# Condition tiles loaded a step ahead from GpSimd's queue, and gate one-hots built for eight tokens per instruction, in a three-layer transformer kernel

## The chip, the core and the metric

The kernel runs on one core of a Trainium2 chip. The core has a matrix engine (TensorE, PE in the rows), a vector engine (VectorE, DVE), an engine for activation functions (ScalarE, ACT), GpSimd (POOL), and SyncE (SP), which here issues most of the transfers. Each engine runs its own instructions in the order in which they stand. They wait for each other through semaphores. The metric is the device time of one execution in microseconds (us), and the median of several executions is the kernel's time.

## What is computed

Three layers run over 256 tokens of width 1024. The first two take a gain, a shift and a gate from a condition vector `c`, and the third ends in a product-key expert layer. Cut to what matters:

```python
cond = jax.nn.silu(c)
for i in range(2):
    mod = (cond @ ada_w[i] + ada_b[i]).reshape(B, 6, D)      # 6144 numbers per layer
    h = rms_norm(x, norm_mix[i]) * (1 + scale1) + shift1
    x = x + gate1 * (mla_mixer(h) if i == 0 else dilated_mixer(h))
    h = rms_norm(x, norm_mlp[i]) * (1 + scale2) + shift2
    x = x + gate2 * (jnp.square(jax.nn.relu(h @ mlp_w1[i])) @ mlp_w2[i])
# third layer: recurrence and chunk attention, cross attention, then the experts:
#   8 heads pick 16 of 16384 experts each, number = 128 * i1 + i2, gate = softmax of the scores
act = gelu(einsum('td,tkd->tk', x, expert_u[idx]))
x = x + einsum('tk,tkd->td', gate * act, expert_v[idx])
```

## The kernel before

Weights come from memory as slabs of 128 x 1024 float32 (`slab`, line 264): SP loads a slab into `raw` (4 buffers), ScalarE rounds it to `wH` (line 268), VectorE takes the rest `wL = raw - wH` (line 270), and TensorE multiplies with three matmuls per 128 x 128 block (`mm3`, lines 275 to 277). A linear step of 1024 inputs and 128 outputs is one slab and 24 matmuls. An engine can be at most four slabs ahead, since `raw`, `wH` and `wL` have four buffers each.

**Condition tiles.** `cond @ ada_w` is not done on TensorE. The transposed weights lie as 48 tiles of 128 x 1024 per layer (512 KB each). One tile gives 128 of the 6144 numbers: `ada_tile` (line 458) loads the tile into `araw`, multiplies it with `cond` (the same in every row) and sums along the row. That is one instruction on VectorE (line 465), or, for tiles marked `pool_too`, a multiply on GpSimd (line 462) and a summing copy on ScalarE (line 463). There are 96 tiles. The first 16 are worked off in the start, with 8 buffers of their own. The other 80 share two `araw` buffers and are handed out as "aside" steps: 24 in the latent attention (`mla`, half of them through GpSimd), 24 in the first MLP (all but one on VectorE), 24 in the dilated attention (`dil`, half through GpSimd) and 8 in the second MLP (half). Their loads go through `late` (line 259), which puts a load on SP's queue and tells the scheduler to keep it behind the slab that was asked for last. Load and sum of a tile are written in one step.

Beside these tiles the first MLP also hides the bias tables of `dil` (`t5`, line 788): 20 transfers `br` issued by GpSimd bring bucket numbers in, VectorE compares them (`oh`, line 853), TensorE looks the bias up (lines 861, 862), and ScalarE's queue stores it.

**Experts.** All 128 x 128 expert columns are computed densely. `up(n2)` is one slab of `expert_u`: 24 matmuls and a gelu. The gates are spread out to a 128 x 128 table per token by a matmul of two one-hot matrices: for each token t and each of the 128 selections, `A` marks the first key number and `B` holds the gate at the second key number, in two float16 parts. This *build* goes over 4 quarters of 64 tokens and in each over 8 chunks of 8 tokens (`TC = 8`): 24 small VectorE instructions per chunk (lines 1532 and 1534), 16 matmuls (line 1539), two evictions into `G` (line 1540). A finished quarter is stored to memory in 8 pieces from ScalarE's queue (line 1547). `fill(us)` places `up` steps into the build: one per 1.5 of the sum of its arguments. Then follows the *value stage*: gate pieces `GG` are loaded back (line 1565), and `gw`, `gaH`, `gaL` (lines 1575 to 1580) are multiplied with slabs of `expert_v` into `v`. Its first matmul needs the stored gates of all four quarters.

**Order.** The program is written as nested loops, but a scheduler that keeps a model of the timing picks the order of the instructions on each engine, within the bounds of dependences, buffers and such hints as `late`. Once built, the order is fixed: an instruction that waits holds up everything behind it on its engine.

Of the kernel before, what the change touches and what calls it, by code (L numbers as in the profile page):

```python
# [11 lines left out]
F32 = mybir.dt.float32  # L12
F32R = mybir.dt.float32r
BF = mybir.dt.bfloat16
F16 = mybir.dt.float16
# [6 lines left out]
T = 256  # L22
# [197 lines left out]
def program(ctx: ExitStack, tc, I, out, co):  # L220
# [234 lines left out]
                nc.tensor.matmul(p[:, k], sel[:, 512 * n + 128 * k:512 * n + 128 * k + 128], e, start=True, stop=True)  # L455
            evict(cond[:, 512 * n:512 * n + 512], p.rearrange("p a b -> p (a b)"))

    def ada_tile(l, j, pool_too=False, tp=None, bufs=2, behind=False):
        raw = (tp or ada_pool).tile([128, 1024], F32, name="araw", bufs=bufs)
        (late if behind else dma)(raw, I["adaT"][l, j])  # L460
        if pool_too:
            nc.gpsimd.tensor_tensor(raw, raw, cond, op=OP.mult)  # L462
            nc.scalar.activation(raw, raw, AF.Copy, accum_out=MOD[l][:, j:j + 1])
            return
        nc.vector.tensor_tensor_reduce(raw, raw, cond, scale=1.0, scalar=0.0, op0=OP.mult, op1=OP.add,  # L465
                                       accum_out=MOD[l][:, j:j + 1])

    def ada_end(l, part):
        s = slice(8 * part, 8 * part + 8)
        nc.vector.tensor_add(MOD[l][:, s], MOD[l][:, s], cc(f"ada_b{l}", 8 * part, 8))  # L470
        if part % 3 == 1:
            n = ("norm_mix", "norm_mlp")[part // 3]
            o = slice(8 * (part // 3), 8 * (part // 3) + 8)
            nc.vector.scalar_tensor_tensor(GA[l][:, o], MOD[l][:, s], 1.0, cc(f"{n}{l}", 0, 8),
                                           op0=OP.add, op1=OP.mult)

    def ada_steps(l, parts, pool_of=2):
        for part in parts:
            for j in range(8 * part, 8 * part + 8):
                ada_tile(l, j, j % pool_of == 0, behind=True)  # L480
                if j % 8 == 7:
                    ada_end(l, part)
                yield

    def mod_normed(l, half):
        with pool("psn", space=PS) as pn:
# [134 lines left out]
    def mla(sin, cos, X, r):  # L621
        with pool("mla") as mp:
# [3 lines left out]
            with pool("mlap") as lp, pool("psacc", 5, space=PS) as pa, pool("psss", space=PS) as ps:  # L626
# [8 lines left out]
                kr = lp.tile([128, T], F32, name="kr")  # L635
                XQ = [lp.tile([128, 3, T], F32R, name="xq" + s) for s in "HL"]
                XK = [lp.tile([128, 2, T], F32R, name="xk" + s) for s in "HL"]
                tiles = iter(range(16, 40))

                def aside(n):  # L640
                    for _ in range(n):
                        j = next(tiles, None)
                        if j is None:
                            return
                        ada_tile(0, j, j % 2 == 0, behind=True)
                        if j % 8 == 7:
                            ada_end(0, j // 8)

                w = I["w_mla_in"]
                for m in (3, 4, 0, 1, 2):  # L650
# [714 lines left out]
    def peer(Xq, done):  # L1365
# [11 lines left out]
        X = normed(xt, 8, r, lambda k: cc("norm_ffn", k), pair())  # L1377
        pre.close()
        with pool("peer") as mp, pool("psp", 2, space=PS) as ps:
            iT = [mp.tile([128, T], F32, name=f"iT{j}") for j in range(3)]  # L1380
            g16 = mp.tile([128, T], F16, name="g16")
            gp = [mp.tile([128, T], F32, name=f"gp{j}") for j in range(2)]
            iota = mp.tile([128, 128], F16, name="iota")
            io = mp.tile([128, 128], F32, name="io")
            dma(io, I["iota"])
# [31 lines left out]
            with pool("route") as rp, pool("psr", space=PS) as pr:  # L1417
# [51 lines left out]
                def gates(t):  # L1469

                    e = got[t][2].rearrange("p (a b) -> p a b", a=8)
                    nc.vector.tensor_sub(e, tops[t], tops[t][:, :, 0:1].to_broadcast([128, 8, 16]))
                    nc.scalar.activation(e, e, AF.Exp)
                    su = rp.tile([128, 8], F32, name="su", bufs=2)
                    nc.vector.reduce_sum(su, e, axis=AX.X)
                    nc.vector.reciprocal(su, su)
                    nc.vector.tensor_mul(e, e, su[:, :, None].to_broadcast([128, 8, 16]))
                    s = slice(128 * t, 128 * t + 128)
                    for j in range(3):
                        p = pr.tile([128, 128], F32, name="tr", bufs=1)  # L1480
                        nc.tensor.transpose(p, got[t][j], ident)
                        nc.scalar.activation(iT[j][:, s], p, AF.Copy, scale=(1.0, 1.0, 2.0 ** 15)[j])

                    nc.vector.tensor_copy(g16[:, s], iT[2][:, s])
                    nc.vector.tensor_copy(gp[0][:, s], g16[:, s])
                    nc.vector.tensor_sub(gp[1][:, s], iT[2][:, s], gp[0][:, s])
                    fill(1.5)

# [34 lines left out]
            with pool("build") as bt, pool("psb", space=PS) as pb:  # L1523
                for q in range(NQ):
                    G = bt.tile([128, 128, TQ], F32, name="G", bufs=2)
                    for c in range(TQ // TC):
                        A = bt.tile([128, TC, 128], F16, name="A", bufs=2)
                        B = bt.tile([128, TC, 2, 128], F16, name="Bg", bufs=2)
                        for j in range(TC):
                            t = TQ * q + TC * c + j  # L1530
                            col = lambda v: v[:, t:t + 1]
                            nc.vector.tensor_scalar(A[:, j], iota, col(iT[0]), None, op0=OP.is_equal)
                            for i in range(2):
                                nc.vector.tensor_scalar(B[:, j, i], iota, col(iT[1]), col(gp[i]), op0=OP.is_equal, op1=OP.mult)  # L1534
                        for j in range(0, TC, TP):
                            p = pb.tile([128, TP, 128], F32, name="gb", bufs=4)
                            for k in range(TP):
                                for i in range(2):
                                    nc.tensor.matmul(p[:, k], A[:, j + k], B[:, j + k, i], start=i == 0, stop=i == 1)
                            nc.scalar.activation(G[:, :, TC * c + j:TC * c + j + TP], p.rearrange("p t n -> p n t"), AF.Copy,  # L1540
                                                 scale=2.0 ** -15)
                        if stores:
                            stores.pop(0)()
                        fill(3.7)

                    def store(q, G, n):
                        return lambda: nc.scalar.dma_start(gd[q, :, n:n + SN], G[:, n:n + SN])  # L1547

                    stores += [store(q, G, n) for n in range(0, 128, SN)]
                for n2 in todo:  # L1550
                    up(n2)
                    if stores:
                        stores.pop(0)()
                while stores:
                    stores.pop(0)()
# [90 lines left out]
    with pool("start") as start:  # L1646
# [3 lines left out]
        def between():  # L1650
            k = next(n)
            for j in (k, 8 + k):
                ada_tile(0, j, j < 8, start, 8)
                nc.vector.tensor_add(MOD[0][:, j:j + 1], MOD[0][:, j:j + 1], cc("ada_b0", j))
            nc.vector.scalar_tensor_tensor(GA[0][:, k:k + 1], MOD[0][:, 8 + k:9 + k], 1.0, cc("norm_mix0", k),
                                           op0=OP.add, op1=OP.mult)
# [47 lines left out]
```

## Time and profile before

| | us |
|---|---|
| median of 3 executions | 2071.1 (2070.01 to 2071.22) |
| the profiled execution | 2070.24 |
| its span, from the first instruction to the last | 2068.5 |
| TensorE busy in the span | 1945.3 (94%) |
| VectorE busy | 1582.8 (77%) |
| ScalarE busy | 1195.7 (58%) |
| GpSimd busy | 194.5 (9%) |

Busy shares are averages over stages of different kinds. Matmuls overlap, so a busy TensorE need not run at its peak. A stage is judged by what TensorE waits for in it, and by the engine that is behind that wait. Windows below are in us from the start of the span. The latent attention and its output end at about 222, the first MLP runs to about 457, `dil` to about 830, the second MLP begins there, the build runs from 1410 to 1663, and the value stage from about 1697 to the end.

### The profile page before, as it was taken

How to read it: one execution, taken by the hardware profiler on the slowest of the kernel's cores; microseconds unless marked ns; L12 is line 12 of the kernel's file. 1: busy time of each engine (PE TensorE's matmuls, PEld its weight loads, DVE VectorE, ACT ScalarE, POOL GpSimd, SP SyncE). 2: the span in 40 equal slices, each digit the busy share in tenths (PEclk: the TensorE clock that was granted, in tenths of full speed). 3: DMA queues.
4: the chain of work that ended last, by engine and by line, in shares of the span. 5: the costliest groups of instructions: out<-in, count | busy, mean ns of one | idle time of the engine just before them, and what ended most of it. 6: DMA issues, size and time to landing. Idle time of an engine off the chain costs nothing.

```text
span 2068.5 us, 36918 instructions
## 1 busy us (share of the span) xinstructions
PE 1945.3 (94%) x13516; PEld 1755.7 (85%) x13516; DVE 1582.8 (77%) x3606; ACT 1195.7 (58%) x2270; POOL 194.5 (9%) x156
## 2 busy tenths in 40 slices
PE   6988998888999999999999999999999979999998
PEld 5765998887878787999987999998899968888886
DVE  8877885547776876875588679999999947777676
ACT  4855676335775675695466565554455535555554
POOL 4112111111221210300100110000000000000000
PEclk8998999999999999999999999999999989999999
DMA  8663588777645643665554545554677788888674
GB/s 322 224 224 112 205 252 242 252 249 238 227 163 166 204 133 102 233 198 190 190 198 134 204 144 174 179 173 155 246 242 246 275 284 283 293 292 287 226 243 143
DMA packets 170247, 441.91 MB, mean 214 GB/s; under 512 B 20705, under 2 KB 74745, under 8 KB 169425
## 3 DMA queue, kind: packets, MB, share of 16 engines
q1 hardware_dynamic: 158064, 409.99, 59.8%
q10 hardware_dynamic: 6480, 24.12, 3.0%
q0 software_dynamic: 5520, 5.44, 1.1%
q8 instruction: 106, 1.74, 0.3%
q14 instruction: 77, 0.62, 0.1%
HBM read 398.40 MB, written 37.91 MB: 211 GB/s over the span
## 4 chain that ended last, share of the span: by engine, by line
PE 71%; DMA 9%; DVE 9%; ACT 4%; issue 3%; ACTq 1%; SPq 0%; POOL 0%; DVEq 0%; POOLq 0%
PE acc L275 16%; PE acc L277 15%; PE acc L276 15%; DMA araw<-in_adaT 6%; PE v L275 6%; PE v L276 6%; PE v L277 6%; DVE wL L270 3%; ACT wH L268 1%; ACTq L1547 1%; DVE Bg L1534 1%; DVE araw L465 1%; PE S L938 1%; PE acc L921 1%; PE acc L590 1%
## 5 line engine op out<-in xcount | busy, mean ns | idle before, releaser
L268 ACT ACTIVATE wH<-raw 128x1024 fp32r<-128x1024 f32 x565 | 595.8, 1058 | 443.9 <-PE acc L276 285.6
L270 DVE TENSOR_TENSOR wL<-raw,wH 128x1024 fp32r<-128x1024 f32 x565 | 700.7, 1245 | 176.8 <-ACT wH L268 157.1
L275 PE MATMUL acc<-hH,wH 128*128 128x256 f32 (+1 forms) x2168 | 628.6, 290 | 15.4 <-ACT gs L1401 7.8
L276 PE MATMUL acc<-hL,wH 128*128 128x256 f32 (+1 forms) x2168 | 619.6, 286 | 5.9 <-DVE hL L394 5.3
L277 PE MATMUL acc<-hH,wL 128*128 128x256 f32 (+1 forms) x2168 | 616.6, 285 | 1.8 <-DVE wL L270 1.8
L275 PEld LDWEIGHTS acc<-hH,wH 128*128 128x128 f32 x2168 | 413.9, 191 | 24.8 <-ACT gs L1401 9.5
L276 PEld LDWEIGHTS acc<-hL,wH 128*128 128x128 f32 x2168 | 413.1, 191 | 9.1 <-DVE hL L394 6.1
L277 PEld LDWEIGHTS acc<-hH,wL 128*128 128x128 f32 x2168 | 412.7, 191 | 3.9 <-DVE wL L270 2.5
L275 PE MATMUL v<-wH,gaH 128*128 128x512 f32 x512 | 200.4, 391 | 13.3 <-ACT gaH L1579 13.3
L276 PE MATMUL v<-wL,gaH 128*128 128x512 f32 x512 | 200.2, 391 | 0.0
L277 PE MATMUL acc<-hidH,wL 128*128 128x256 f32 x512 | 146.4, 286 | 11.0 <-DVE wL L270 11.0
L465 DVE CUSTOM_DVE_ANT_0 araw<-araw,cond 128x1024 f32<-128x1024 f32 x59 | 83.5, 1416 | 95.2 <-DMA araw<-in_adaT 95.2
L275 PE MATMUL acc<-hidH,wH 128*128 128x256 f32 x512 | 145.6, 284 | 1.0 <-ACT wH L268 1.0
L276 PE MATMUL acc<-hidL,wH 128*128 128x256 f32 x512 | 145.6, 284 | 0.0
L277 PE MATMUL v<-wH,gaL 128*128 128x512 f32 x512 | 140.7, 390 | 0.0
L1534 DVE TENSOR_SCALAR Bg<-iota,iT,gp 128x128 f16<-128x128 f16 x512 | 138.5, 309 | 0.0
L462 POOL TENSOR_TENSOR araw<-araw,cond 128x1024 f32<-128x1024 f32 x37 | 92.7, 2506 | 350.7 <-DMA araw<-in_adaT 301.4
L275 PEld LDWEIGHTS v<-wH,gaH 128*128 128x128 f32 x512 | 96.7, 189 | 33.4 <-ACT gaH L1579 13.5
L1579 ACT ACTIVATE gaH<-gw 128x256 fp32r<-128x256 f32 x128 | 53.4, 418 | 115.7 <-PE v L276 97.4
L277 PEld LDWEIGHTS v<-wH,gaL 128*128 128x128 f32 x512 | 96.6, 189 | 20.3
L276 PEld LDWEIGHTS v<-wL,gaH 128*128 128x128 f32 x512 | 96.7, 189 | 19.9
L277 PEld LDWEIGHTS acc<-hidH,wL 128*128 128x128 f32 x512 | 98.8, 193 | 12.4 <-DVE wL L270 12.2
(447 smaller groups left out, 3385.5 us busy)
## 6 DMA issues: line engine op xcount, KB each, us to landing
raw<-in_w SPq DMA_DIRECT2D x128, 512.0 KB
raw<-in_uT SPq DMA_DIRECT2D x128, 512.0 KB
raw<-in_v SPq DMA_DIRECT2D x128, 512.0 KB
araw<-in_adaT SPq DMA_DIRECT2D x96, 512.0 KB
gd<-G ACTq DMA_DIRECT2D x32, 512.0 KB
GG<-gd SPq DMA_DIRECT2D x32, 512.0 KB
raw<-in_w_dv SPq DMA_DIRECT2D x24, 512.0 KB
raw<-in_w_dq SPq DMA_DIRECT2D x24, 512.0 KB
```

The lines of the kernel that those rows point to most:

```text
L268: nc.scalar.activation(H, raw, AF.Copy)
L270: (lo or nc.vector).tensor_sub(L, raw, H)
L275: kept(nc.tensor.matmul(p, aH, bH, start=start, stop=False))
L276: kept(nc.tensor.matmul(p, aH, bL, start=False, stop=False))
L277: kept(nc.tensor.matmul(p, aL, bH, start=False, stop=stop))
L462: nc.gpsimd.tensor_tensor(raw, raw, cond, op=OP.mult)
L465: nc.vector.tensor_tensor_reduce(raw, raw, cond, scale=1.0, scalar=0.0, op0=OP.mult, op1=OP.add, accum_out=MOD[l][:, j:j + 1])
L590: nc.tensor.matmul(p, KB[:v[i].shape[0], 128 * j:128 * j + 128], v[i], start=i == 0, stop=i == 1)
L921: nc.tensor.matmul(p[:, 1], k2("b64"), square(p[:, 0]), start=True, stop=True)
L938: nc.tensor.matmul(Ss[i][:, t], pm(q[rows], t), kt, start=True, stop=True)
L1534: nc.vector.tensor_scalar(B[:, j, i], iota, col(iT[1]), col(gp[i]), op0=OP.is_equal, op1=OP.mult)
L1579: nc.scalar.activation(aH, w, AF.Copy)
```

## The change

The load of a tile and its sum become two functions. `ada_steps` asks for the load of the next tile before it sums the present one, and issues it from GpSimd's queue, no longer through `late`. The handing out in `mla` now goes through `ada_steps` too. The 16 tiles of the start stay on SP's queue.

In the build the 24 instructions of a chunk become four over all eight tokens (8 x 128 elements): two comparisons and two products. In each, one operand is a token's number or gate, repeated along the innermost dimension. The tiles `iT` and `gp` become float16 where they were float32, and a helper tile is dropped. `fill` is given 2.8 per chunk in place of 3.7.

```diff
-    def ada_tile(l, j, pool_too=False, tp=None, bufs=2, behind=False):
+    def ada_load(l, j, tp=None, bufs=2, q=None):
         raw = (tp or ada_pool).tile([128, 1024], F32, name="araw", bufs=bufs)
-        (late if behind else dma)(raw, I["adaT"][l, j])
+        (q or dma)(raw, I["adaT"][l, j])
+        return raw
+
+    def ada_sum(l, j, raw, pool_too=False):
         if pool_too:
             nc.gpsimd.tensor_tensor(raw, raw, cond, op=OP.mult)
             nc.scalar.activation(raw, raw, AF.Copy, accum_out=MOD[l][:, j:j + 1])
...
     def ada_steps(l, parts, pool_of=2):
-        for part in parts:
-            for j in range(8 * part, 8 * part + 8):
-                ada_tile(l, j, j % pool_of == 0, behind=True)
-                if j % 8 == 7:
-                    ada_end(l, part)
-                yield
+
+        js = [j for part in parts for j in range(8 * part, 8 * part + 8)]
+        raw = {}
+        for n, j in enumerate(js):
+            for k in js[n:n + 2]:
+                if k not in raw:
+                    raw[k] = ada_load(l, k, q=nc.gpsimd.dma_start)
+            ada_sum(l, j, raw[j], j % pool_of == 0)
+            if j % 8 == 7:
+                ada_end(l, j // 8)
+            yield
...
-                tiles = iter(range(16, 40))
+                tiles = ada_steps(0, (2, 3, 4))
...
-            iT = [mp.tile([128, T], F32, name=f"iT{j}") for j in range(3)]
-            g16 = mp.tile([128, T], F16, name="g16")
-            gp = [mp.tile([128, T], F32, name=f"gp{j}") for j in range(2)]
+            iT = [mp.tile([128, T], F16 if j < 2 else F32, name=f"iT{j}") for j in range(3)]
+            gp = [mp.tile([128, T], F16, name=f"gp{j}") for j in range(2)]
...
-                        for j in range(TC):
-                            t = TQ * q + TC * c + j
-                            col = lambda v: v[:, t:t + 1]
-                            nc.vector.tensor_scalar(A[:, j], iota, col(iT[0]), None, op0=OP.is_equal)
-                            for i in range(2):
-                                nc.vector.tensor_scalar(B[:, j, i], iota, col(iT[1]), col(gp[i]), op0=OP.is_equal, op1=OP.mult)
+                        s = slice(TQ * q + TC * c, TQ * q + TC * c + TC)
+                        inner = lambda v: v[:, s, None].to_broadcast([128, TC, 128])
+                        numbers = iota[:, None, :].to_broadcast([128, TC, 128])
+                        eq = bt.tile([128, TC, 128], F16, name="eqb", bufs=1)
+                        nc.vector.tensor_tensor(A, numbers, inner(iT[0]), op=OP.is_equal)
+                        nc.vector.tensor_tensor(eq, numbers, inner(iT[1]), op=OP.is_equal)
+                        for i in range(2):
+                            nc.vector.tensor_tensor(B[:, :, i], eq, inner(gp[i]), op=OP.mult)
...
-                        fill(3.7)
+                        fill(2.8)
```

The built order moves with it, since loads are no longer held behind slabs. In the first MLP GpSimd's queue before held the bucket transfers in a row (`br`), after one condition sum:

```order
L462 TENSOR_TENSOR araw<-araw,cond 128x1024
L832 DMA buck_d_2417<-bb 128x384
L833 DMA buck_d_2418<-bb 128x256
L849 DMA br<-buck_d_2417 128x1x1024 x12
L849 DMA br<-buck_d_2418 128x1x1024 x5
L386 TENSOR_TENSOR ssq<-ssq,sq 128x256
```

The same place now (`L460` is a tile's load, `L465` a tile's multiply on GpSimd):

```order
L835 DMA buck_d_2419<-bb 128x384
L836 DMA buck_d_2420<-bb 128x256
L460 DMA araw<-in_adaT 128x1024
L465 TENSOR_TENSOR araw<-araw,cond 128x1024
L852 DMA br<-buck_d_2419 128x1x1024 x3
L460 DMA araw<-in_adaT 128x1024 x2
L852 DMA br<-buck_d_2419 128x1x1024 x2
L465 TENSOR_TENSOR araw<-araw,cond 128x1024
L852 DMA br<-buck_d_2419 128x1x1024
L460 DMA araw<-in_adaT 128x1024 x2
```

Loads and multiplies of tiles now stand among the bucket transfers. The tiles that `dil` and the second MLP handed out have moved into the first MLP, and no tile is left behind its 55th slab or so. On VectorE in the latent attention there was one condition sum (`L465`) in every two or three heads, among the softmax steps (`mx`, `ng`, `sums`, `P`):

```order
L565 TENSOR_REDUCE mx<-acc 128x2
L567 TENSOR_SCALAR ng<-mx 128x2
L574 RECIPROCAL sums<-sums 128x2
L465 ISA araw,mod_92<-araw,cond 128x1024
L465 ISA mod_92 128x1
L576 TENSOR_SCALAR P<-P,sums 128x256 x2
L565 TENSOR_REDUCE mx<-acc 128x2
L574 RECIPROCAL sums<-sums 128x2
L363 TENSOR_TENSOR xqL<-o,xqH 128x256
```

There now (`L468` is the sum):

```order
L468 ISA araw,mod_92<-araw,cond 128x1024
L468 ISA mod_92 128x1
L573 TENSOR_REDUCE mx<-acc 128x2
L468 ISA araw,mod_92<-araw,cond 128x1024
L468 ISA mod_92 128x1
L575 TENSOR_SCALAR ng<-mx 128x2
L573 TENSOR_REDUCE mx<-acc 128x2
L582 RECIPROCAL sums<-sums 128x2
L575 TENSOR_SCALAR ng<-mx 128x2
L584 TENSOR_SCALAR P<-P,sums 128x256 x2
L573 TENSOR_REDUCE mx<-acc 128x2
L468 ISA araw,mod_92<-araw,cond 128x1024
```

From the first `mx` to the first row of the output projection there were 6 sums, and now there are 20: those of the first MLP have moved here. On VectorE in the build the row was of small instructions with a `wL` among them:

```order
L270 TENSOR_TENSOR wL<-raw,wH 128x1024
L1532 TENSOR_SCALAR A<-iota,iT_14121 128x128
L1534 TENSOR_SCALAR Bg<-iota,iT_14122,gp_14125 128x128
L1534 TENSOR_SCALAR Bg<-iota,iT_14122,gp_14126 128x128
L1532 TENSOR_SCALAR A<-iota,iT_14121 128x128
```

and is now

```order
L1534 TENSOR_TENSOR A<-iota,iT_14121 128x1024
L1537 TENSOR_TENSOR Bg<-eqb,gp_14124 128x8x128
L1537 TENSOR_TENSOR Bg<-eqb,gp_14125 128x8x128
L270 TENSOR_TENSOR wL<-raw,wH 128x1024
L1535 TENSOR_TENSOR eqb<-iota,iT_14122 128x1024
L270 TENSOR_TENSOR wL<-raw,wH 128x1024
```

Two `wL` stand in most chunks, where before it was two or three.

## Rows read from the trace of the kernel before

**Rows 1.** The page, its first part: busy time, share of span, instructions.

```profile
PE 1945.3 (94%) x13516; PEld 1755.7 (85%) x13516; DVE 1582.8 (77%) x3606; ACT 1195.7 (58%) x2270; POOL 194.5 (9%) x156
```

**Rows 2.** Windows by stage: length; PE, PEld, DVE, ACT, POOL busy; clock; DMA; GB/s.

```profile
0.00:57.00 57.00, 36.83 (x202) 32.91 (x202) 50.32 (x87) 30.90 (x57) 21.29 (x16) 0.85 0.82 311
...
222.00:457.00 235.00, 212.98 (x1606) 204.55 (x1605) 158.70 (x244) 130.35 (x248) 27.61 (x31) 0.95 0.78 248
...
475.00:830.00 355.00, 345.37 (x2248) 289.43 (x2249) 261.30 (x646) 238.13 (x565) 66.93 (x51) 0.97 0.52 171
...
1410.00:1663.00 253.00, 242.38 (x2188) 234.66 (x2187) 238.50 (x842) 124.33 (x203) 0.00 (x0) 0.99 0.68 233
1663.00:1701.00 38.00, 24.72 (x193) 23.58 (x192) 11.77 (x15) 12.35 (x22) 0.00 (x0) 0.83 0.90 324
```

**Rows 3.** VectorE's waits in the whole span: total, times, longest.

```profile
DVE araw L465 <- DMA araw<-in_adaT: 95.2, 30, 8.6
```

**Rows 4.** VectorE's waits in the first MLP, 222 to 457.

```profile
DVE araw L465 <- DMA araw<-in_adaT: 67.7, 15, 8.6
```

**Rows 5.** Timeline of SP and of VectorE, 355 to 400: start, duration, what.

```profile
357.02 0.42 SPq L262 DMA_DIRECT2D araw<-in_adaT  x1
...
368.16 1.23 DVE L465 CUSTOM_DVE_ANT_0 araw<-araw,cond 128x1024 f32<-128x1024 f32 x1 [8.62 <-DMA araw<-in_adaT]
```

**Rows 6.** The chain that ended last: start, duration, what. Loads in it.

```profile
167.23 5.84 DMA araw<-in_adaT
...
440.88 9.01 DMA araw<-in_adaT
...
466.81 5.97 DMA araw<-in_adaT
...
839.59 5.99 DMA araw<-in_adaT
```

**Rows 7.** Groups of instructions by line (busy us, mean ns | idle before, releaser).

```profile
L462 POOL TENSOR_TENSOR araw<-araw,cond 128x1024 f32<-128x1024 f32 x37 | 92.7, 2506 | 350.7 <-DMA araw<-in_adaT 301.4 <-ACT P L571 17.8 <-ACT mnH L1262 9.3
L463 ACT ACTIVATE araw<-araw 128x1024 f32<-128x1024 f32 x37 | 39.0, 1054 | 31.0 <-POOL araw L462 31.0
L849 POOL DMA_DIRECT2D br<-buck_d x20 | 13.6, 683 | 95.9 <-DVE oh L853 84.9 <-DMA br<-buck_d 7.6 <-issue 3.3
```

**Rows 8.** DMA issues: queue, count, size, median us from issue to landing.

```profile
br<-buck_d POOLq DMA_DIRECT2D x20, 256.0 KB, 11.9
```

**Rows 9.** One tile, `araw`: duration ns min/median/max, first and last start.

```profile
L465 DVE CUSTOM_DVE_ANT_0 araw<-araw,cond x59: 1208/1226/3405, 14.7 to 862.2; 128x1024 f32<-128x1024 f32 x59
```

**Rows 10.** Shorter windows, columns as in rows 2: start, attention and after it.

```profile
30.00:40.00 10.00, 3.33 (x24) 2.93 (x24) 9.86 (x20) 4.72 (x6) 5.35 (x3) 0.81 1.03 408
...
140.00:200.00 60.00, 46.48 (x197) 29.48 (x198) 48.25 (x114) 35.19 (x105) 14.08 (x6) 0.83 0.50 163
200.00:210.00 10.00, 10.00 (x65) 8.07 (x62) 1.18 (x4) 1.53 (x5) 0.00 (x0) 0.83 0.01 2
```

**Rows 11.** Timeline of VectorE inside the build.

```profile
1505.95 1.22 DVE L270 TENSOR_TENSOR wL<-raw,wH 128x1024 fp32r<-128x1024 f32 x1
1507.09 0.25 DVE L1532 TENSOR_SCALAR A<-iota,iT 128x128 f16<-128x128 f16 x1
1507.25 0.53 DVE L1534 TENSOR_SCALAR Bg<-iota,iT,gp 128x128 f16<-128x128 f16 x2
1507.70 0.24 DVE L1532 TENSOR_SCALAR A<-iota,iT 128x128 f16<-128x128 f16 x1
```

**Rows 12.** Two other VectorE lines: of 1024 elements each.

```profile
L1462 DVE TENSOR_TENSOR eq<-ra,const x4: 1218/1219/1223, 1287.2 to 1384.9; 128x1024 f32<-128x1024 f32 x4
...
L853 DVE TENSOR_SCALAR oh<-br,const 128x1024 fp32r<-128x1024 bf16 x20 | 15.4, 772 | 3.1 <-DMA br<-buck_d 3.0
```

**Rows 13.** A window of `up` steps alone on TensorE, columns as in rows 2.

```profile
1250.00:1300.00 50.00, 50.00 (x421) 50.00 (x420) 48.88 (x236) 24.70 (x42) 0.00 (x0) 1.00 0.56 180
```

**Rows 14.** TensorE's waits, 1663 to 1705: total, times, longest.

```profile
PE v L275 <- ACT gaH L1579: 13.3, 1, 13.3
```

More of the change, by code (lines that the diff above doesn't have):

```diff
@@ L637, in mla @@
                 XK = [lp.tile([128, 2, T], F32R, name="xk" + s) for s in "HL"]
-                tiles = iter(range(16, 40))
+                tiles = ada_steps(0, (2, 3, 4))
                 def aside(n):
                     for _ in range(n):
[L642 to L647, printed above, removed]
+                        next(tiles, None)
                 w = I["w_mla_in"]
@@ L1482, in gates @@
                         nc.scalar.activation(iT[j][:, s], p, AF.Copy, scale=(1.0, 1.0, 2.0 ** 15)[j])
-                    nc.vector.tensor_copy(g16[:, s], iT[2][:, s])
-                    nc.vector.tensor_copy(gp[0][:, s], g16[:, s])
+                    nc.vector.tensor_copy(gp[0][:, s], iT[2][:, s])
                     nc.vector.tensor_sub(gp[1][:, s], iT[2][:, s], gp[0][:, s])
@@ L1652, in between @@
             for j in (k, 8 + k):
-                ada_tile(0, j, j < 8, start, 8)
+                ada_sum(0, j, ada_load(0, j, start, 8), j < 8)
                 nc.vector.tensor_add(MOD[0][:, j:j + 1], MOD[0][:, j:j + 1], cc("ada_b0", j))
```

## The prediction

> **What bounds the kernel now.** I read the page's busy times first, then the windows by stage, then the waits in each stage, then the chain that ended last, and single rows last. TensorE is busy 94% of the span [rows 1], so a change gains only where TensorE idles, where its clock is low, or where it works slower than it could behind another engine. In the first MLP it is busy 213.0 of 235 us at clock 0.95; in `dil` 345.4 of 355; in the build 242.4 of 253; between build and value stage 24.7 of 38 [rows 2]. VectorE waits for condition tiles 95.2 us in 30 waits [rows 3], 67.7 of them in 15 waits in the first MLP [rows 4]. One such wait in full: SP issues the load at 357.02, and VectorE stands 8.62 us in front of the sum until 368.16 [rows 5]. Every `wL` behind that sum is late by as much. That the waits reach TensorE shows in the chain: four loads of tiles lie on it, one in the attention (5.84), one late in the first MLP (9.01), one at the start of `dil` (5.97) and one at the start of the second MLP (5.99) [rows 6]. In the build VectorE is busy 238.5 of 253 us [rows 2], almost as full as TensorE.
>
> The sum is made against the profiled execution (2070.24, of which the span is 2068.5); the median of the runs, 2071.1, lies 0.9 above it.
>
> **Start: +7 (0 to +13).** The built order draws some six loads of tiles, two or three sums on VectorE and three multiplies on GpSimd into the start. Where the start is full the transfers run at 1.03 of their share and 408 GB/s, and VectorE is busy 9.86 of 10 us [rows 10]. Six loads of 524 KB at 408 GB/s are 6 x 1.28 = 7.7 us; I take 7. Over all 57 us the share is 0.82 [rows 2], so they may fit in at nothing; three sums beside GpSimd, at somewhere between the median 1.23 and the longest 3.41 [rows 9], could add some 5 more.
>
> **Latent attention: +6 (-4 to +20).** It gets 14 sums more on VectorE (20 for 6), 14 x 1.23 = 17 us [rows 9]. VectorE idles 11.7 of 60 us in the attention and 8.8 of 10 behind it [rows 10]. With 20 as the upper end (17 and 3 of delay between them), I let a third show, since VectorE there works between short waits of the softmax; without its load on the chain (5.84 [rows 6]) it could gain 4.
>
> **First MLP: -7 (-33 to +47).** It loses 23 sums on VectorE with their waits, and gets the 32 tiles of `dil` and the second MLP, as 16 pairs, 15 of them between its 35th and 87th slab counted from the kernel's first; the bucket transfers `br` stand among 9 of these. A pair is one tile for VectorE and one for GpSimd, and the two buffers make it a ring: GpSimd's multiply (2.51), ScalarE's summing copy (1.05), an issue on GpSimd (0.68 [rows 7]), the landing. The landing is the unknown. The rows have 5.84 to 5.99 where little else runs and 9.01 late in the first MLP [rows 6], and 11.9 for `br` on GpSimd's own queue, though those are other transfers, of 256 KB [rows 8]. I take 9.01 among the `br`, the one row on a tile there, and 5.97 elsewhere. A pair among `br` then takes 2.51 + 1.05 + 0.68 + 9.01 = 13.3 us, elsewhere 10.2. TensorE's own time for the 52 slabs between is 52 x 213.0 / 64 = 173 us [rows 2], 11.5 per pair. So 6 pairs go at 11.5 and 9 at 13.3, 188 in all, and the other 12 slabs take 12 x 3.33 = 40: 228 in place of 235. The floor is TensorE's 213 (-22), or -33 if its clock also rose from 0.95 to 1. What is queued behind a sum that waits on VectorE: the `wL` of the next slabs, up to four of which TensorE has in store, and then the tile compares `oh`. Behind GpSimd's waiting multiply: the next loads and the `br`, on which `oh` and the bias matmuls hang.
>
> [...]
>
> **Later stages: -16 (0 to -28).** The start of `dil` no longer waits for a tile, a chain step of 5.97 [rows 6]: -5 (0 to -9). `dil` itself loses 24 tiles; TensorE idles 9.6 us there, and clock 0.97 costs at most 0.03 x 345 = 10 [rows 2]. VectorE is relieved of 12 sums, 14.7 us [rows 9], and of waits (27.5 outside the first MLP, 95.2 less 67.7 [rows 3, 4]): -8 (0 to -14). The second MLP: half of the step of 5.99 [rows 6], -3 (0 to -5). What is late next there is TensorE itself.
>
> **Build and handover: -11 (+1 to -24).** A token's `A` and two `Bg` start 0.61 us apart from the next token's (1507.09 to 1507.70) [rows 11], 4.9 us for a chunk of eight. The new row is four instructions of 1024 numbers. The nearest row by form is `eq`, a two-operand compare of 1024, 1.219 us [rows 12]: 4 x 1.22 = 4.9, the same. A `wL` starts 1.14 after its start (1505.95 to 1507.09) [rows 11], and four at this pace make 4.56. So the 32 chunks take VectorE 146 to 156 us, where it was 156: the larger instructions save at most 10. The price from the other side is `oh`, with 16-bit input, 0.772 [rows 12], 99 us for 128; but it has one tensor operand, the new ones two, so I take `eq`. The second effect is `fill`: 2.8 for 3.7 gives about 64 `up` in the build for 72, each `wL` at 1.14. VectorE needs 146 to 156 and 73, 219 to 229; TensorE needs 242.4 less 7.5 x 2.85 = 221, one `up` being 24 matmuls at 50 us for 421 [rows 13]. The build ends after some 232 (with 8 us of idle, today's being 10.6 on TensorE) in place of 253: -21. The 7.5 `up` are not gone. Four more stand between the last gate matmul and the first `v`, where TensorE waits 13.3 us for `gaH` [rows 14] in a handover of 38 us [rows 2]: 11.4 us of work that fits. The other 3.5 cost 3.5 x 2.85 = 10. So -11; +1 if VectorE stays as slow as it is and `up` cover nothing more, -24 at `oh`'s price.
>
> Sum: 7 + 6 - 7 - 16 - 11 = -21, so 2049 for the profiled execution and 2050 for the median.
>
> **Rivals.** (1) *The pairs run as fast as TensorE*: loads that are ahead land in 5.97 also among the `br`. The cycle of 10.2 is then hidden behind 11.5, and the first MLP takes 213: -22 for -7, 2035. For it: the loads no longer stand behind slabs on SP. Against: 9.01 at the same load of the queues [rows 6].
>
> (2) *The one-hots run at twice the rate*, `oh`'s 0.77 for 1.22 [rows 12]: the build falls to TensorE's 221, -21 for -11, 2040. For it: all operands are 16 bits wide, `eq`'s are not. Against: no two-operand row in 16 bits is there. [...]
>
> (3) *GpSimd's queue turns the pairs round too slowly* (slower): GpSimd works in order, so the load of the tile after next is issued only behind its own multiply, and lands 11.9 after it as `br` do [rows 8]. A pair takes 16.1 us. With the 9 pairs among `br` the first MLP takes 9 x 16.1 + 69 + 40 = 254, +19, the whole 2076; with all 15, 282, +47, the whole 2104. The kernel is no faster than before from a cycle of 13.9 in all 15 pairs, a landing of 9.7. For it: the row of the same queue. Against: the tiles' own landings of 5.8 to 9.0 [rows 6].
>
> (4) *The pulled-in work is paid in full*: start and attention cost 13 and 20 for my 7 and 6, 2070, no change. For it: VectorE is full in the start [rows 10]. Against: its idle time in the attention.
>
> **How the numbers follow.** About 0.2%, 4 us, is what a measurement can tell from no change. Forecast 0.50 (2050, its own range 2035 to 2072; 0.06 of it within 4 us of before). Rival 1 0.18, rival 2 0.12, both faster. Rival 3 0.12, slower. Rival 4 0.08, of which 0.04 same and 0.02 on either side. Faster 0.44 + 0.18 + 0.12 + 0.02 = 0.76, same 0.06 + 0.04 = 0.10, slower 0.14. The range: rivals 1 and 2 together give 2025, with a part of the clock 2022; above, 2086 takes in rival 3's nine pairs and 10 us more. Outside lie rival 3 with all pairs and the last of rival 1, under 2 in 10.
>
> **What the profile after would show.** In the first MLP, VectorE's wait for `araw`: under 40 us for 67.7 if I am right, near nothing in rival 1, over 100 in rival 3; loads of tiles landing in 6 and 9 us, against 12. No `araw` wait at all in `dil`. The start ending near 64 for 57, the attention some 6 longer. The four build instructions at 1.2 us each, or 0.7 in rival 2. TensorE's wait for `gaH` falls from 13.3 to a few us. What would make the prediction wrong above all: the order of the condition tiles. They share two buffers, so one late tile holds the next, and with them the slabs behind it on VectorE.

## The result, and the profile after

The changed kernel took 2101.5 us (2089.7 to 2103.3 in 4 runs), 1.0136 times the kernel before (95% interval 1.0115 to 1.0158): 28 us slower by this ratio, 30 by the medians, where 21 us faster was forecast. Its profiled execution spans 2099.7 us, 31.2 more than before.

Where the 31.2 us are is read from the tiles' own rows. Each gives duration in ns (min/median/max), then the first and the last start; the tile, not the line number, is to be compared. The kernel after:

```profile
L1277 DVE TENSOR_TENSOR ko<-acc,rm x8: 412/424/425, 33.4 to 82.5; 128x256 f32<-128x256 f32 x8
...
L573 DVE TENSOR_REDUCE mx<-acc x16: 667/680/692, 167.2 to 220.2; 128x2 f32<-128x512 f32 x16
...
L856 DVE TENSOR_SCALAR oh<-br,const x20: 739/750/1219, 338.0 to 486.0; 128x1024 fp32r<-128x1024 bf16 x20
...
L557 DVE CUSTOM_DVE_ANT_0 sb<-S,B x96: 239/286/358, 580.7 to 847.7; 128x128 f32<-128x128 f32 x64, 128x192 f32<-128x192 f32 x32
...
L1534 DVE TENSOR_TENSOR A<-iota,iT x32: 1211/1218/1227, 1448.2 to 1678.5; 128x1024 f16<-128x1024 f16 x32
...
L1542 PE MATMUL gb<-Bg,A x512: 216/219/330, 1457.2 to 1689.4; 128*128 128x128 f16 x171
...
L275 PE MATMUL v<-wH,gaH x512: 387/389/403, 1725.0 to 2090.0; 128*128 128x512 f32 x171
```

The same rows of the kernel before:

```profile
L1274 DVE TENSOR_TENSOR ko<-acc,rm x8: 414/420/425, 28.5 to 62.1; 128x256 f32<-128x256 f32 x8
...
L565 DVE TENSOR_REDUCE mx<-acc x16: 662/680/692, 146.3 to 193.0; 128x2 f32<-128x512 f32 x16
...
L853 DVE TENSOR_SCALAR oh<-br,const x20: 743/748/1236, 303.7 to 432.8; 128x1024 fp32r<-128x1024 bf16 x20
...
L549 DVE CUSTOM_DVE_ANT_0 sb<-S,B x96: 239/286/358, 533.1 to 803.9; 128x128 f32<-128x128 f32 x64, 128x192 f32<-128x192 f32 x32
...
L1532 DVE TENSOR_SCALAR A<-iota,iT x256: 235/249/264, 1410.0 to 1662.3; 128x128 f16<-128x128 f16 x128
...
L1539 PE MATMUL gb<-Bg,A x512: 216/219/233, 1414.7 to 1672.2; 128*128 128x128 f16 x171
...
L275 PE MATMUL v<-wH,gaH x512: 387/389/792, 1697.3 to 2058.8; 128*128 128x512 f32 x171
```

The table sets them side by side. The last gate matmul (`gb`) ends the build on TensorE.

| mark | before | after | behind by | since the mark above | predicted |
|---|---|---|---|---|---|
| last `ko` (the start) | 62.1 | 82.5 | 20.4 | +20.4 | +7 |
| last `mx` (attention) | 193.0 | 220.2 | 27.2 | +6.8 | +6 |
| last `oh` (first MLP, bias tables) | 432.8 | 486.0 | 53.2 | +26.0 | -7 |
| first `sb` (start of `dil`) | 533.1 | 580.7 | 47.6 | -5.6 | -5 |
| first `A` (`dil`, second MLP and on) | 1410.0 | 1448.2 | 38.2 | -9.4 | -11 |
| last `gb` (build) | 1672.2 | 1689.4 | 17.2 | -21.0 | -21 |
| first `v` (handover) | 1697.3 | 1725.0 | 27.7 | +10.5 | |
| last `v` with `gaH` | 2058.8 | 2090.0 | 31.2 | +3.5 | +10, with the row above |

Two of the terms failed, the start and the first MLP; between them they miss by 46 us, the rest by 6. The `wL` of the 87th slab, near the end of the tiles, starts 52.4 us later than before (476.3 for 423.9), so the last `oh` has not merely changed its place among the slabs.

**The start.** The timeline of GpSimd, then a row of VectorE and one of TensorE (start, duration, instruction, wait before it and what ended that):

```profile
45.72 0.58 POOL L460 DMA_DIRECT2D araw<-in_adaT  x1 [12.67 <-ACT araw L466]
...
54.55 0.58 POOL L460 DMA_DIRECT2D araw<-in_adaT  x1 [5.87 <-DVE mod L468]
55.15 9.27 POOL L465 TENSOR_TENSOR araw<-araw,cond 128x1024 f32<-128x1024 f32 x4
...
54.84 10.65 DVE L468 CUSTOM_DVE_ANT_0 araw<-araw,cond 128x1024 f32<-128x1024 f32 x1
...
67.90 0.58 PE L277 MATMUL acc<-mnH,wL 128*128 128x256 f32 x1 [10.59 <-DVE wL L270]
```

Two loads of tiles stand 12.67 and 5.87 us in GpSimd's queue until a buffer is free, and the start's multiplies stand behind them. When the second load is out, four multiplies run in a row for 9.27 us. A VectorE sum beside them takes 10.65 us, where one takes 1.22 and the longest of before took 3.41 [rows 9]. All of VectorE stands behind that sum, and TensorE waits 10.59 us for the next `wL`.

**The first MLP.** GpSimd's timeline: the multiply just ahead of the first bucket transfers, one turn of the two buffers, and the last multiply of a tile:

```profile
328.73 2.55 POOL L465 TENSOR_TENSOR araw<-araw,cond 128x1024 f32<-128x1024 f32 x1 [2.16 <-DMA araw<-in_adaT]
...
381.05 2.36 POOL L465 TENSOR_TENSOR araw<-araw,cond 128x1024 f32<-128x1024 f32 x1 [6.68 <-DMA araw<-in_adaT]
383.36 0.69 POOL L852 DMA_DIRECT2D br<-buck_d  x1
386.33 0.57 POOL L460 DMA_DIRECT2D araw<-in_adaT  x1 [2.28 <-DVE mod L468]
...
392.93 0.72 POOL L852 DMA_DIRECT2D br<-buck_d  x1 [3.68 <-DVE oh L856]
...
398.34 2.90 POOL L465 TENSOR_TENSOR araw<-araw,cond 128x1024 f32<-128x1024 f32 x1 [2.29 <-DMA araw<-in_adaT]
...
471.31 2.83 POOL L465 TENSOR_TENSOR araw<-araw,cond 128x1024 f32<-128x1024 f32 x1
```

The queue waits in turn for a tile to land, for a buffer, and for `oh` to give back a `br`. The multiplies at 328.73 and 471.31 are the first and the last of nine, so there are eight turns between them, 17.8 us each. The seven turns ahead of them, where no `br` is under way, took 10.4 us each, near the 10.2 that the forecast took there. The landings of tiles asked for from 290 to 470, from the rows on the tile:

```profile
DMA to landing us min/median/max: 3.7/11.5/21.3
```

11.5 in the median is near rival 3's 11.9, not the 9.01 that the forecast took. What VectorE waited for there (250 to 480: total us, times, longest):

```profile
DVE araw L468 <- DMA araw<-in_adaT: 45.5, 9, 15.7
DVE oh L856 <- DMA br<-buck_d: 20.3, 8, 6.5
```

The wait for tiles fell from 67.7 us [rows 4] to 45.5, nearly what was forecast (under 40), but `oh` now waits 20.3 us for buckets, where it was 3.0 [rows 12]: 65.8 together for 70.7.

So VectorE's waits are no longer than they were, and the stage is. TensorE's waits show more. First one of its waits before (222 to 457), then the same one after (250 to 480), and a wait of ScalarE's after:

```profile
PE t5acc L861 <- ACT ob L863: 3.8, 2, 2.3
```

```profile
PE t5acc L864 <- ACT ob L866: 13.6, 6, 3.9
...
ACT araw L466 <- POOL araw L465: 51.6, 15, 11.0
```

TensorE waits 13.6 us for `ob`, ScalarE's copies of the bias tables, and 16.0 for `wL`, where it was 10.2. In ScalarE's queue the summing copies now wait 51.6 us for GpSimd's multiplies; before there was one such copy in this stage, and it waited 1.7. `ob` and `wH` stand behind them. Thus three queues stand behind late tiles, GpSimd's, VectorE's and ScalarE's. No run tells ScalarE's share from that of the two buffers.

**The build.** One of the instructions of a chunk as a group (busy us, mean ns | idle before), a piece of VectorE's timeline, and TensorE's waits from 1430 to 1745:

```profile
L1537 DVE TENSOR_TENSOR Bg<-eqb,gp 128x1024 f16<-128x1024 f16 x64 | 75.3, 1217 | 0.1
...
1506.78 1.22 DVE L1534 TENSOR_TENSOR A<-iota,iT 128x1024 f16<-128x1024 f16 x1 [0.20 <-PE gb L1542]
1507.92 2.35 DVE L1537 TENSOR_TENSOR Bg<-eqb,gp 128x1024 f16<-128x1024 f16 x2
```

```profile
PE acc L275 <- ACT gs L1403: 16.5, 10, 4.1
```

1.217 us each: the price taken from `eq` [rows 12], so rival 2 fell. The next one starts 1.14 us after (1506.78 to 1507.92), the lower end of the forecast's range. The wait of 13.3 us for `gaH` [rows 14] is gone, as forecast. In its place `up` waits 16.5 us for ScalarE's `gs`, the results of `up` on their way to memory, which have two buffers. Before it was 7.8, all of it ahead of the last `Bg`; now 8.1 of the 16.5 are behind it.

### The profile page after: what moved, and what is told of

It is laid out like the page before. It is cut to its first block, busy times and chain, and to the rows that moved or that the text cites. A ratio compares the mean times of both kernels' runs of the same rounds, so it can differ in the third digit from the quotient of the medians.

```text
span 2099.7 us, 36289 instructions
## 1 busy us (share of the span) xinstructions
PE 1947.8 (93%) x13516; PEld 1758.5 (84%) x13516; DVE 1576.2 (75%) x2964; ACT 1198.8 (57%) x2270; POOL 240.1 (11%) x236
## 4 chain that ended last, share of the span: by engine, by line
PE 73%; DMA 10%; DVE 6%; issue 4%; ACT 2%; POOL 2%; ACTq 1%; SPq 0%; DVEq 0%; POOLq 0%
PE acc L275 16%; PE acc L277 16%; PE acc L276 16%; PE v L275 6%; PE v L276 6%; PE v L277 6%; DMA araw<-in_adaT 5%; DMA br<-buck_d 3%; POOL araw L465 2%; DVE wL L270 1%; DVE araw L468 1%; ACTq L1550 1%; PE gb L1542 1%; PE S L941 1%; PE acc L924 1%
## 5 line engine op out<-in xcount | busy, mean ns | idle before, releaser
L270 DVE TENSOR_TENSOR wL<-raw,wH 128x1024 fp32r<-128x1024 f32 x565 | 710.1, 1260 | 230.2 <-ACT wH L268 211.7
L275 PE MATMUL acc<-hH,wH 128*128 128x256 f32 (+1 forms) x2168 | 629.0, 290 | 22.3 <-ACT gs L1403 16.5
L468 DVE CUSTOM_DVE_ANT_0 araw<-araw,cond 128x1024 f32<-128x1024 f32 x59 | 84.7, 1436 | 57.8 <-DMA araw<-in_adaT 57.5
L465 POOL TENSOR_TENSOR araw<-araw,cond 128x1024 f32<-128x1024 f32 x37 | 97.6, 2641 | 105.8 <-DMA araw<-in_adaT 97.9
L275 PEld LDWEIGHTS acc<-hidH,wH 128*128 128x128 f32 x512 | 99.6, 195 | 3.1 <-ACT wH L268 2.0
```

The source lines that it names most:

```text
L270: (lo or nc.vector).tensor_sub(L, raw, H)
L275: kept(nc.tensor.matmul(p, aH, bH, start=start, stop=False))
```

## The experiments

Ratios are to the kernel before on the same chip, with 95% intervals. Single runs of one kernel differ by up to 1.0% here (before: 2064.7 to 2084.7 in the second of three sets), so a profile's span can lie 10 us off its kernel's median.

**The two parts apart.** First the build alone (the condition tiles as before), then the condition tiles alone (the build as before).

> The kernel before with the build part of the change alone (wide one-hots, 2.8 for 3.7), condition tiles as before. Read from the changed kernel, the stretch from the first A to the first v got 10.5 us shorter and the value stage 3.6 us longer. If the two parts are independent, this kernel stands 7 us under before, about 2064, and spends the span up to the first A as before (1410). If the build's gain in the changed kernel was only a shift of work, it is within 4 us of before.

2067.8 us, 0.9981 (0.9960 to 1.0002): some 4 us faster, not certainly.

> The kernel before with the condition-tile part alone; the build as before. Independent parts give 2071 + 38 = 2109, with the 38 already there at the first A. A median under 2095 would say that the parts work on each other.

2109.3 us, 1.0175 (1.0139 to 1.0210), some 36 us slower. The two add up to 32 us where 28 were measured, which agrees within the intervals, so nothing shows that the parts work on each other. The loss is all in the condition tiles.

**Place or queue.** The loads stay one step ahead on GpSimd's queue, but the sums are held at their places of before, behind the `wL` written last:

```diff
-            ada_sum(l, j, raw[j], j % pool_of == 0)
+            with tc.issue_after(last_rest[0]):
+                ada_sum(l, j, raw[j], j % pool_of == 0)
```

> The condition-tile part alone, with loads one step ahead from GpSimd's queue, but each sum is put behind the wL that was written last before it on VectorE's queue, so that the sums stand near their places of before (20 in the attention become 6 again, and tiles are handed out in dil and in the second MLP). Theory place (the tiles were pulled forward into start, attention and first MLP, and that costs the 38 us): 2055 to 2072, the wait of VectorE for tiles falling from 95 us. Theory queue (GpSimd's in-order queue turns the two buffers round too slowly, and its multiplies run in trains, wherever the tiles stand): 2085 to 2105, with the first MLP still over 245 us long.

2083.7 us, 1.0060 (1.0043 to 1.0077): between the ranges of the two theories, and from the last `mx` to the last `oh` it took 228.9 us, less than the 239.8 of before. And the loads on SyncE's queue, the sums pulled forward:

```diff
-                    raw[k] = ada_load(l, k, q=nc.gpsimd.dma_start)
+                    raw[k] = ada_load(l, k)
```

> The condition-tile part alone, loads one step ahead but from SyncE's queue, not held behind slabs; the sums are pulled forward nearly as in the changed kernel (20 in the attention, the last behind slab 85). Theory place: 2095 to 2115. Theory queue: 2065 to 2080. That both are needed would give something between, 2080 to 2095.

2096.6 us, 1.0129 (1.0093 to 1.0166), in the range of theory place. But the 27 us can't be read as the price of place alone. SyncE's queue, from which the slabs are loaded, now stands behind tile loads that wait for a free buffer. SyncE's waits, and the row of `ko`:

```profile
SPq L460 <- DVE mod L468: 56.0, 24, 7.1
...
L1277 DVE TENSOR_TENSOR ko<-acc,rm x8: 413/422/425, 28.4 to 67.6; 128x256 f32<-128x256 f32 x8
```

The start tells the queues apart. In this run loads are pulled into the start too, but SyncE issues them, and the start ended 5.5 us late, not 20.4, with no sum over 3.5 us. With held sums on GpSimd's queue the last `ko` stood at 74.0, 11.9 us late. There three multiplies run in a row behind a load that stood 7.60 us, and beside them VectorE's `hn`, which takes 0.28 us elsewhere, takes 7.28:

```profile
44.84 6.94 POOL L468 TENSOR_TENSOR araw<-araw,cond 128x1024 f32<-128x1024 f32 x3
...
L616 DVE TENSOR_SCALAR hn<-hn x2: 280/3782/7283, 44.7 to 51.9; 128x256 f32<-128x256 f32 x2
```

**The start kept clear.** Each of GpSimd's loads is queued behind the multiply that was written last, which for the first of them is the start's last one. One run has the sums where the change has them, the other holds them:

```diff
+    def behind_start(o, i):
+        with tc.issue_after(last_mult[0]):
+            nc.gpsimd.dma_start(o, i)
...
-                    raw[k] = ada_load(l, k, q=nc.gpsimd.dma_start)
+                    raw[k] = ada_load(l, k, q=behind_start)
```

> The condition-tile part alone as changed, but GpSimd's loads are queued behind the eighth and last multiply of the start. Theory train (a load that waits for a buffer on GpSimd holds the start's multiplies, four then run in a row and one VectorE sum beside them takes 10.65 us): the start no longer loses 18 us, 2091 to 2098, and no sum is over 4 us long. Theory work (the pulled-in tiles cost their own time wherever they are put): the loss comes back behind the start, 2104 to 2112.

2086.8 us, 1.0078 (1.0049 to 1.0107): some 20 us of the 36 come back, more than expected. The rows of `ko` and of the sums:

```profile
L1283 DVE TENSOR_TENSOR ko<-acc,rm x8: 414/424/426, 28.2 to 66.9; 128x256 f32<-128x256 f32 x8
...
L474 DVE CUSTOM_DVE_ANT_0 araw<-araw,cond x59: 1202/1224/3433, 14.5 to 481.6; 128x1024 f32<-128x1024 f32 x59
```

The start ends at 66.9 instead of 82.5, and the longest sum takes 3.43 us instead of 10.65. That is 15 us. Another 12 come back in the first MLP: from the last `mx` to the last `oh` this run is 13.8 us behind the kernel before, the tiles alone 26.1. The later stages give some 7 of that up again. Why a clear start spares the first MLP 12 us isn't settled. With the sums held as well:

> The run with held sums and GpSimd loads (2084, of which 12 us were lost by the eighth slab), with GpSimd's loads also queued behind the start's last multiply. Theory train: 2068 to 2076, as before the change. If GpSimd's queue costs the 12 us in any place: 2080 to 2088.

2075.2 us, 1.0019 (0.9999 to 1.0040): as before, or up to 8 us slower. So with a clear start the pulled-in tiles cost the difference, 1.0078 to 1.0019, some 12 us. VectorE's waits in this run (whole span):

```profile
DVE oh L866 <- DMA br<-buck_d: 29.5, 7, 9.3
...
DVE araw L477 <- DMA araw<-in_adaT: 11.9, 6, 3.6
```

The wait for tiles has gone from 95.2 us [rows 3] to 11.9. A third of what went is now a wait for buckets (29.5 us, where it was 3.0 [rows 12]), and the kernel is no faster. In the first MLP it did gain: by the marks of its tiles, the last `mx` to the last `oh` takes 228.2 us (203.2 to 431.4) against 239.8 before, 11.6 less. But start and attention are 10 us late, of which the attention, with its sums at their old places, makes 5.5. Then the stretch to the first `sb` takes 108.5 against 100.3, and from the first to the last `sb` 276.8 against 270.8: 14 us more. In the first of these TensorE's clock was granted at 0.91 against 0.95. What makes `dil` slower there isn't settled. One candidate, untested, is that SyncE's slab loads now wait for the stores of the bias tables, 45.0 us where it was 9.5:

```profile
SPq L267 <- DMA bias_d<-ob: 45.0, 8, 9.8
```

**One step ahead by itself.** The loads stay on SyncE behind their slab:

```diff
-                    raw[k] = ada_load(l, k, q=nc.gpsimd.dma_start)
+                    raw[k] = ada_load(l, k, q=late)
```

> The condition-tile part alone with the loads one step ahead, but on SyncE's queue behind the slab asked for last, as before; the sums stand at their places of before. This is one step ahead by itself. If VectorE's wait of 95 us for tiles was worth what the prediction took (some 20 us in the first MLP and behind it), 2045 to 2060. If it covered other waits (the run with held sums cut it to 12 us and was not faster), within 6 us of before, 2066 to 2078.

2072.4 us, 1.0011 (0.9991 to 1.0031). As before, but this does not say what a step ahead is worth, for in the order that was built the loads hardly moved. In the first MLP (sums that start from 230 to 440) they were issued 8.6 us ahead of their sums in the median, 8.8 before, and 8 of 21 ahead of the sum of the tile before, where it was 6. With held sums and a clear start it is 18.0 us, and 21 of 22. So the wait is nearly as long as it was (whole span):

```profile
DVE araw L468 <- DMA araw<-in_adaT: 87.1, 34, 8.9
```

**What sets the pace in the first MLP.** Both runs start from the one with the clear start (1.0078). In one, the 32 tiles of the later stages are all summed on VectorE (`pool_of` 64), so that the buffers no longer turn through GpSimd's multiply and ScalarE's copy:

```diff
-    X = dil(ada_steps(1, (2, 3, 4)))
-    X = mlp(1, X, ada_steps(1, [5]), g=lambda k: cc("norm_mix2", k))
+    X = dil(ada_steps(1, (2, 3, 4), 64))
+    X = mlp(1, X, ada_steps(1, [5], 64), g=lambda k: cc("norm_mix2", k))
```

> The run with the start kept clear, but the 32 tiles of dil and the second MLP are all summed by VectorE, so that GpSimd's multiply (2.5 us) and ScalarE's copy (1.05) are out of the ring of two buffers; VectorE gets 16 sums more, 16 x 1.23 = 20 us, in the first MLP. Theory ring (the turn of the two buffers through GpSimd sets the pace): the first MLP 8 to 20 us shorter, 0 to 0.4% over before. Theory VectorE (the work that was pulled in sets the pace there): longer by up to 20 us, 1.0 to 1.7% over before.

2086.1 us, 1.0082 (1.0052 to 1.0111), the same in total, but not inside. Matmuls with `wL` on VectorE's rows, 290 to 380 and 380 to 480 (length; PE, PEld, DVE busy with their counts, the last of which is the number of slabs; clock; DMA; GB/s). The first of the two windows, with pairs and then with VectorE alone:

```profile
290.00:380.00 90.00, 49.52 (x168) 34.09 (x168) 31.02 (x23) 0.89 0.86 254
```

```profile
290.00:380.00 90.00, 62.64 (x224) 42.50 (x223) 33.07 (x28) 0.98 0.95 293
```

Without the ring 28 slabs pass in the first 90 us in place of 23, and then, from 380 to 480, 19 in place of 25. VectorE's waits from 290 to 480 tell why; again with pairs, then without:

```profile
DVE araw L474 <- DMA araw<-in_adaT: 35.2, 7, 10.6
DVE oh L862 <- DMA br<-buck_d: 19.9, 9, 6.0
```

```profile
DVE oh L862 <- DMA br<-buck_d: 38.6, 13, 7.9
...
DVE araw L474 <- DMA araw<-in_adaT: 12.6, 8, 3.5
```

55.1 us and 51.2: the tiles' wait falls from 35.2 to 12.6, so the turn through GpSimd and ScalarE did hold VectorE, as rival 3 has it, but with it gone the buckets hold it. The run also takes the copies out of ScalarE's queue; it doesn't tell the two apart. In the other run `br` is issued by SyncE:

```diff
-                    nc.gpsimd.dma_start(br[n], bass.AP(...))
+                    dma(br[n], bass.AP(...))
```

> The run with the start kept clear (0.8% over before, tiles still pulled into the first MLP), with the bucket transfers br issued by SyncE instead of GpSimd. Theory shared queue (br wait behind the tiles' loads and multiplies on GpSimd, and the tile compares and bias tables behind them): the first MLP gets 8 us shorter or more, the kernel within 0.4% of before. Theory tiles (the pairs themselves, or the transfers' load, set the pace): within 3 us of the run with the start kept clear, 0.7 to 0.9% over before.

2120.3 us, 1.0248 (1.0218 to 1.0278), 34 us worse than the run it starts from, and the last `oh` stands 34 us later than there (493.7 for 459.5). SyncE stands 28.9 us in front of issues of `br`, with the slabs behind them, and TensorE waits for the bias tables; SyncE's and TensorE's waits in the whole span:

```profile
SPq L858 <- DMA br<-buck_d: 28.9, 7, 6.3
```

```profile
PE t5acc L870 <- ACT ob L872: 39.9, 8, 10.3
```

An issue that waits held up SyncE's queue here as it held up GpSimd's.

**The build.** The wide instructions with the filling of before, then 2.8 and 3.3 with four buffers for `gs`:

```diff
-                        fill(2.8)
+                        fill(3.7)
```

> The build part alone with the filling of before, 3.7. The one-hot instructions take 1.217 us each in the changed kernel, 4 x 1.217 = 4.87 us per chunk for 4.88 before, so by the instructions alone this is within 4 us of before, and the 4 to 6 us of the build part come from the filling. If the wide instructions give the gain, 2064 to 2068.

2063.2 us, 0.9955 (0.9928 to 0.9981). The expectation from the instructions' durations fell: by their starts, 1.14 us apart, a chunk is some 0.3 us cheaper, and from the first `A` to the last `gb` this run takes 254.5 us for 262.2. So the wide instructions give a gain by themselves. That 2.8 gives some of it back is likely, but the intervals of the two runs (0.9928 to 0.9981 and 0.9960 to 1.0002) overlap. TensorE's waits from 1395 to 1740 with 2.8, then with 3.7:

```profile
PE acc L275 <- ACT gs L1400: 21.7, 10, 5.4
```

```profile
PE v L275 <- ACT gaH L1579: 12.3, 1, 12.3
PE acc L275 <- ACT gs L1400: 4.0, 5, 1.1
```

By TensorE's matmuls, with 2.8 some three `up` more are left for the handover (7.4 for 4.0) and two more behind the first `v`; the wait for `gaH` goes, but `gs` takes 21.7 us for 4.0.

```diff
-                    a = mp.tile([128, T], F32, name="gs", bufs=2)
+                    a = mp.tile([128, T], F32, name="gs", bufs=4)
```

> The build part alone (2.8) with four buffers for gs, the results of up that go to memory, in place of two. In the build part alone TensorE waited 21.7 us for ACT gs, 9.6 of it in the handover, where SyncE's queue holds the stores of gs behind slab loads. Theory gs: that wait falls under 6 us, and the kernel stands 0.5 to 1.1% under before. If the handover is bound by the gates on their way through memory in any case, it stays at 0.2% under before.

2068.8 us, 0.9986 (0.9968 to 1.0005). A miss:

```profile
PE v L275 <- ACT gaH L1579: 18.0, 1, 18.0
```

The wait for `gs` fell to 9.4 us, by half, but with more buffers the scheduler moved the `up` out of the handover into the build, and the wait for `gaH` is back. The same with 3.3:

```diff
-                        fill(2.8)
+                        fill(3.3)
```

> The same with 3.3 in place of 2.8: some four up more in the build and fewer in the handover. Theory gs: 0.5 to 1.0% under before, with part of the 13 us wait for gaH back. If 3.7 was better than 2.8 because the handover needs no up at all: between the two, 0.3 to 0.5% under.

2059.1 us, 0.9945 (0.9924 to 0.9966), with 17.8 us of waiting for `gaH` and 1.3 for `gs`. This is the fastest version, with the condition tiles as before: some 11 us under the kernel before. It can't be told from the run with 3.7 and two buffers, and beats both kernels as that one does.

## Why the prediction was wrong

**The start, +7 for +20.4.** The step that failed is the sum of transfers and sums. It priced what was added, with a sum beside GpSimd at 3.41 us at most, and did not follow what the new loads do to the instructions behind them on GpSimd. The prediction says that a queue's later instructions wait behind a waiting load, but for the first MLP alone. Shown by the run with the clear start: without loads among the start's multiplies it ends 15 us earlier. That the row of multiplies is the mechanism is read from the rows: three in a row held a VectorE instruction for 7.28 us, four for 10.65, and with single multiplies no sum is longer than 3.43. The run with loads from SyncE agrees, late by 5.5 us, near the +7 that was priced.

**The attention, +6 for +6.8.** The number came out. Its cause isn't shown: that a third of the added sums shows was a choice, and in the two runs with the sums held at their old places the attention was still 2.0 and 5.5 us longer. The agreement is in part luck.

**The first MLP, -7 for +26.0.** The step that failed is the turn of a pair among the `br`: 13.3 us were taken, and it took 17.8. The landing was taken at 9.01 from the one row on a tile there, and was 11.5; why it is so long isn't settled. The other 2 us are waits in GpSimd's queue, for buffers and for `oh`, which the term put at nothing though it names the `br` behind a waiting multiply. With 17.8 for 13.3 in nine pairs the forecast's own sum gives +34. What it said of waits, that an end to them gains in this stage, isn't refuted: the run with held sums and a clear start gained 11.6 us there. But of the 83 us of waiting that went, the kernel as a whole kept nothing. Rival 3 had the right sign and place, with a chance of 0.12 against the forecast's 0.50; its price for this stage (+19 to +47) holds the measured +26. That its whole (2076 to 2104) holds the measured 2101.5 is luck, since it has the start at +7. And its ring is only one of the bounds: with the ring taken out the buckets held VectorE, and the kernel was no faster.

**Later stages, -16 for -15.0.** Right: the start of `dil` gains 5.6 for 5, the rest 9.4 for 11. It does not make up for where the tiles went.

**Build and handover, -11 for -7.0.** The build itself came out (-21.0 for -21), and so did the price of the wide instructions (1.217 us, not 0.77). In 16 bits and with a repeated number they take what `eq` takes in 32 bits (1.219 [rows 12]). No run has them without the repeated number, so why they stay above `oh`'s 0.77 [rows 12] isn't shown. The mis-sized step is that of the moved `up`: that four of them fit into the wait for `gaH` at no cost. The wait did go, but `up` in a row there wait for `gs`; handover and value stage got 14.0 us longer, where 10 was taken. The instructions do save time, near the 10 us that the forecast took as the most: with 3.7 kept the kernel is 0.45% faster.

The parts: a clear start gives back 20 of the 36 us of the condition tiles, held sums 12 of what is left, and about 4 remain, which can't be told from none. In the other order, held sums give 24 and the clear start then 8. So the two work on each other, and neither number is the price of one alone. With the -4 of the build that is 32, where 28 was measured.

## What to carry to other kernels

A load that is issued from a compute engine's queue carries its wait for a buffer with it (here 12.67 and 5.87 us in GpSimd's queue in the start): before moving one, read which of that engine's instructions will stand behind it, in every stage that the scheduler may pull it into, the start above all. A long wait in a profile is worth only the distance to the next one: here 83 us less of waiting for tiles gave 11.6 us in its stage, where buckets came next, and nothing in the whole. Whether a run moved what it was meant to move is read from its own rows: asking a step earlier behind the slab hardly moved a load. Parts of a change want to be measured apart: the loss of one half hid the gain of the other.

## What the runs showed of the hardware

Twice a VectorE instruction beside GpSimd multiplies in a row ended only behind the last of them: beside four, a sum of two inputs took 10.65 us (1.22 in the median), and beside three, `hn` took 7.28 (0.28 the other time). Beside two (27.34, 5.71 us together, in the changed kernel) a sum that began at 27.25 took 1.22, and where the multiplies stood singly no sum took more than 3.43. The two long VectorE rows begin 0.31 and 0.1 to 0.2 us before those of the multiplies (54.84 and 55.15, 44.7 and 44.84). So by the rows VectorE began first and was held all the same, over several instructions. Why it was held, they don't show.

The 80 tile loads issued by GpSimd landed after 5.1 us in the median and 21.3 at most over the whole kernel, and after 11.5 in the median from 290 to 470. The median of the whole lies under the 5.84 to 5.99 of SyncE's loads before [rows 6], so these rows do not show that a load is slow for coming from GpSimd's queue. The issues themselves took 0.54 us in the median and 0.80 at most. What makes the landings among the `br` longer, no run tells.
